# Scores of a sparse-attention mixer over 128 rows instead of 64, scalings moved from GpSimd to VectorE, and a shorter skip at the end

## The chip, the cores and the metric

The kernel runs on one core of one Trainium2 chip. Its time is the device time of one launch in microseconds; shown are the median and the spread of several runs. The engines are TensorE (PE; its weight loads are PEld), VectorE (DVE), ScalarE (ACT), GpSimd (POOL) and SyncE (SP), which issues the DMAs.

## The reference

Two layers work on 256 tokens of width 1024, each a mixer and a mixture of 16 experts, with a layer norm behind each. The first mixer (stick-breaking attention beside a state-space model) is not touched. The second is a sparse attention of 16 heads of 64 with 4 groups of keys. It has three branches: compressed blocks, selected blocks, and a window. With 256 tokens all blocks are selected and the window covers everything, so the last two are plain causal attention over their own keys (ks, kw) and values (vs, vw).

```python
scale = d ** -0.5                                  # d = 64
s = jnp.einsum('bqgrd,bkgd->bqgrk', qb, kb).astype(jnp.float32) * scale
s = jnp.where(mask[None, :, None, None, :], s, NEG)
p = jax.nn.softmax(s, axis=-1)
o_w = jnp.einsum('bqgrk,bkgd->bqgrd', p.astype(vb.dtype), vb)
...
g = jax.nn.sigmoid(gate.astype(jnp.float32)).reshape(B, L, G, R, 3).astype(x.dtype)
o = g[..., 0:1] * o_c + g[..., 1:2] * o_s + g[..., 2:3] * o_w
return o.reshape(B, L, H * d) @ w_out
```

The expert layers multiply all 256 tokens with the three matrices of each of the 16 experts (6 MB an expert), gated by the router.

## The kernel before

The large products of the mixers are of 32-bit floats in the type fp32r, with each operand split into a high part, which that type holds, and the low rest; they are the sums of high times high, high times low and low times high. Weights come in tiles of 1 MB (128 x 2048) that SP's queue loads into the buffers of the class `u` (20 of them) as these come free (`issue`, L131 to L148). Other classes are `s` (3), `b2` (15 small ones) and eight banks of PSUM, of which `mm` and `acc` have four each. Temporary tiles take their buffers from the same classes as weights, so that a longer-lived temporary is one weight tile less.

The mixer's attention is the generator `attend` (L1558). Step n computes the scores of head n (`head`, L1490), transposes the probabilities of head n - 2 (`turn_p`, L1525), and on every other step the values of a pair of heads (`values`, L1538). A head has two blocks of queries, t = 0 (128 keys) and t = 1 (256 keys), each for the two branches b at once. The queries are turned (`q_turn`, L1391) for eight heads at a time, into the tiles `qq[0]` and `qq[1]`: rows of 64 with the high part, the other 64 with the low part. So L1504, over 128 rows, gives q_high times k_high plus q_low times k_high in one matmul, since the keys' high part `kk` stands in both halves; L1505 adds q_high times k_low with 64 rows of q and the tiles `kl`; L1506 adds the causal mask through a matmul with the identity in bf16. VectorE then takes the maxima (L1507), ScalarE the exponentials and their sums (L1510), VectorE the reciprocals (L1513) and their product with the gates (L1515). The probabilities are scaled by these: for t = 0 on VectorE (L1522, one instruction a branch, 128x128), for t = 1 on GpSimd (L1519, one for both branches, 128x512). `PSC` holds that choice. `turn_p` transposes both, the first with L1529 and the second with L1535.

The first few steps of the attention lie between other jobs: the projections of the mixer (`mm3`, L203 to L205) and the compressed branch (L1455 to L1482). `q_turn(1)` and `cmp(1)` are called between the steps for heads 7 and 8. Each engine executes its own instructions in order. The calls don't set that order alone: the framework's scheduler lays them out by what they wait for. Buffers are given out in the order of calls.

`body` (L1722) runs the whole network once with a limit of 64 tokens per expert. Then every engine loads the largest count of tokens (L1726) and compares (L1728). If it is over the limit, the body of the `If` computes everything anew without the limit. In the runs here that body is skipped. The end block behind it (L1741) waits for all transfers and lets the engines meet.

Of the kernel before, what the change touches and what calls it, by code (L numbers as in the profile page):

```python
# [19 lines left out]
P = 128  # L20
# [18 lines left out]
WARM0 = 5  # L39
WARM2 = 2  # L40
LAG = 2
PSC = (lambda h: False, lambda h: True)
OV = 3
LATE = (8, 10)
LATE_S = 11
# [6 lines left out]
class K:  # L52
# [17 lines left out]
    def restart(self, full):  # L70

        self.full = full
        self.plan, self.tiles, self.late, self.late_s, self.in_s, self.last = [], [], [], [], [], []
        self.left = []
        self.issued = self.used = 0
        self.cap = 0
        self.rest = self.n0 = None
        self.mark = None
        self.loads = None
        self.behind = self.cut = self.tail = None  # L80
        self.staged, self.to_split, self.ahead = [], 0, 2
# [49 lines left out]
    def issue(self, cap=None):  # L131

        self.cap = self.cap if cap is None else cap
        while self.issued < len(self.plan):
            if self.issued - self.used - sum(self.used <= i < self.issued for i in self.left) >= self.cap:
                break
            if self.issued in self.left:
                self.tiles.append(None)
                self.issued += 1
                continue  # L140
            t = (self.s if self.issued in self.in_s else self.u)()
            n = 1024 if self.issued in self.last else 2048
            for c in range(0, 2048, n):
                d = self.loads = self.nc.sync.dma_start(t[:, c:c + n], self.plan[self.issued][:, c:c + n])
                if self.mark is not None:
                    self.follow(d, self.mark)
            self.tiles.append(t)
            self.issued += 1  # L148

    def issue_late(self):  # L150

        i = self.late.pop(0)
        self.tiles[i] = [self.b2() for _ in range(4)]
        for j, t in enumerate(self.tiles[i]):
            self.nc.sync.dma_start(t, self.plan[i][:, j * 512:j * 512 + 512])

    def issue_s(self):

        i = self.late_s.pop(0)
        self.tiles[i] = t = self.s()  # L160
        self.nc.sync.dma_start(t, self.plan[i])

    def unit(self):
        t = self.tiles[self.used]
# [60 lines left out]
    def pack(self, name, dt, parts, t=None):  # L225

        if t is None:
            t = self.const.tile([P, sum(math.prod(sh) for sh in parts)], dt, name="c_" + name)
            setattr(self, name, t)
        d = self.nc.sync.dma_start(t, self.a[name])  # L230
        if self.loads is not None:
            self.follow(d, self.loads)
        o, r = 0, []
        for sh in parts:
            m = math.prod(sh)
            v = t[:, o:o + m]
            if len(sh) > 1:
                ax = "abcd"[:len(sh)]
                v = v.rearrange(f"p ({' '.join(ax)}) -> p {' '.join(ax)}", **dict(zip(ax, sh)))
            r.append(v)  # L240
            o += m
        return r
# [95 lines left out]
    def ln_transpose(self, li, n, store=None):  # L338

        nc = self.nc  # L340
        hT = self.u([P, KC, T])
        for k in range(KC):
            pt = self.acc() if k in (4, 5) else self.mm()
            for t in range(2):
                nc.tensor.transpose(pt[:, t * P:(t + 1) * P], n[:, t, k * P:(k + 1) * P], self.ident)
            self.scaled(hT[:, k], pt[:, 0:T], li, k, k % 2)
            if store is not None and k % 2:
                nc.sync.dma_start(store[:, k - 1:k + 1], hT[:, k - 1:k + 1])
        return hT

    def scaled(self, o, x, li, k, on_act):
# [305 lines left out]
    def s5_tables(self, load_x, room):  # L657
# [4 lines left out]
        small = lambda t, j: t[:, j * 512:j * 512 + 512].rearrange("p (a r h) -> p a r h", a=NP, r=2)  # L662
        par = us[:, 1344:1392].rearrange("p (x a) -> p x a", x=3)
        c8 = us[:, 1392:1424]
        nc.sync.dma_start(us[:, 1344:1424], self.a["s5_par"])
        load_x()
        bc = ua[:, 0:1024].rearrange("p (x a r h) -> p x a r h", x=2, a=NP, r=2)
        nc.sync.dma_start(bc, self.a["s5_bc"])
        lr, li, ldt = par[:, 0], par[:, 1], par[:, 2]
        cols = us[:, 0:960].rearrange("p (n a) -> p n a", a=NP)  # L670
        ints = us.bitcast(I32)[:, 1424:1456].rearrange("p (n a) -> p n a", a=NP)
# [185 lines left out]
    def s5_kernel(self, ca, bd):  # L857

        nc, s5 = self.nc, self.s5
        nc.gpsimd.memset(bd, 0.0)  # L860
        for g in range(2):
            s = slice(g * 64, g * 64 + 64)
            nc.scalar.activation(bd[s, :, :, g * 16:g * 16 + 16], s5["bb"][s], AF.Copy)
        pk = self.mm()
        for k4 in range(4):
            for ri in range(2):
                for q in range(4):
                    pr = k4 * 4 + q
                    nc.tensor.matmul(pk[q * 32:q * 32 + 32, k4 * P:k4 * P + P], bd[:, pr, ri],
                                     ca[ri][:, pr].rearrange("p d h -> p (d h)"), start=(ri == 0), stop=(ri == 1),  # L870
                                     skip_group_check=True, tile_position=(0, q * 32))
        ks = self.b2([P, 4, P])
        nc.scalar.activation(ks.rearrange("p k n -> p (k n)"), pk, AF.Copy)
        nc.gpsimd.tensor_tensor(ks[:, :, 0:16], ks[:, :, 0:16], self.s5dd, ALU.add)
        kds = []
        for kh in range(2):
            kd = self.drp.tile([16, 16, P], F32, name=f"kd{kh}")
            nc.sync.dma_start(kd.rearrange("h (g k) n -> g h (k n)", g=8),
                                ks[:, kh * 2:kh * 2 + 2].rearrange("p k n -> p (k n)"))
            kds.append(kd)  # L880
        return kds

    def s5_toeplitz(self, kds, kts):

        for kt, kd in zip(kts, kds):
            for j in range(8):
                n = 16 * (8 - j)
                self.nc.sync.dma_start(kt[j * 16:j * 16 + 16, :, P - n:P], kd[:, :, 0:n])

    def s5_transpose(self, x, o):  # L890

# [176 lines left out]
    def mixer0(self):  # L1068
# [5 lines left out]

        def load_x():
            t = self.u()
            half = lambda c: nc.sync.dma_start(t[:, c * 1024:c * 1024 + 1024], self.plan[0][:, c * 1024:c * 1024 + 1024])
            for k in range(0, KC, 2):
                nc.sync.dma_start(xT[:, k:k + 2], self.a["xT"][:, k:k + 2])
                if k == 0:  # L1080
                    half(0)
            half(1)
            self.tiles.append(t)
            self.issued += 1
# [16 lines left out]
        def u_out(j):  # L1101
            def f(ps):
                nc.scalar.activation(uS[:, :, j], ps[:, 0:T].rearrange("p (c i) -> p i c", i=8), AF.Copy)
                if j == 3:
                    ud = self.drp.tile([8, P, P], F32, name="ud")
                    nc.sync.dma_start(ud.rearrange("j a n -> a j n"), uS.rearrange("p j k c -> p j (k c)"))
                    nc.sync.dma_start(U.rearrange("p g k c -> p (g k c)"), ud.rearrange("j (h g) n -> (j h) (g n)", h=16))
            return f

        bbp = [self.u([P, 16, 8, 16]) for _ in range(2)]  # L1110
# [190 lines left out]
    def mixer1(self, hT):  # L1301
# [43 lines left out]
        kk = self.u([P, 2, 2, 2, T], F32R)  # L1345
        vh = self.u([P, 2, 1024])
        V = vh[:, 0].rearrange("p (t n) -> p t n", t=2)
        kl = [self.b2((P, 2, T), F32R) for _ in range(2)]
        rows = (slice(0, 64), slice(64, P))

        turned = {}
# [4 lines left out]
        def k_turn(t):  # L1356
            pt = self.turn(turned["k", t]).rearrange("p (b j) n -> p j b n", b=2)
            n = slice(t * P, t * P + P)
            for c, s in enumerate(rows):
                nc.scalar.activation(kk[s, c, :, :, n], pt[s], AF.Copy)  # L1360
                for j in range(2):
                    v.tensor_tensor(kl[j][s, :, n], pt[s, j], kk[s, c, j, :, n].bitcast(F32), ALU.subtract)
                nc.scalar.activation(kk[rows[1 - c], c, :, :, n], pt[s], AF.Copy)

        js = [self.job_T(xs, window(i)) for i in (1, 2, 3)] + self.jobs_tok(xs, k_out, self.acc)
# [121 lines left out]
        hd = {}  # L1487

        def head(i, c):
            j, s = i // 4, slice(c * 64, c * 64 + 64)  # L1490
            h = i * 2 + c
            if c == 0:
                hd["PT"] = self.u()
            PT = hd["PT"][:, 0:1536].rearrange("p (c b n) -> p c b n", c=2, b=2)[:, c]
# [4 lines left out]
            for t in range(2):  # L1499
# [2 lines left out]
                z3 = z[:, 0:2 * n].rearrange("p (b n) -> p b n", b=2)  # L1502
                q = qq[j][:, c, i % 4, t * P:t * P + P]
                nc.tensor.matmul(z3, q, kk[:, c, j, :, 0:n], start=True, stop=False, skip_group_check=True)  # L1504
                nc.tensor.matmul(z3, q[s], kl[j][s, :, 0:n], start=False, stop=False, skip_group_check=True)  # L1505
                nc.tensor.matmul(z3[:, :, t * P:t * P + P], self.identb, self.caus, start=False, stop=True, skip_group_check=True)  # L1506
                v.tensor_reduce(mx[:, 2 * t:2 * t + 2], z3, AX.X, ALU.max, negate=True)  # L1507
                p_ = self.b2((P, 2, T)) if t else p0
# [5 lines left out]
            s2 = sm.rearrange("p (t b) -> p t b", t=2)  # L1514
            v.tensor_tensor(s2, s2, gt[:, :, h, 1:3], ALU.mult)  # L1515
            for t in range(2):
                x, n, pool = pr[t], P * (t + 1), PSC[t](h)
                if pool:
                    nc.gpsimd.tensor_tensor(x, x, sm[:, 2 * t:2 * t + 2, None].broadcast_to([P, 2, n]), ALU.mult)  # L1519
                    continue  # L1520
                for b in range(2):
                    v.tensor_scalar(x[:, b], x[:, b], sm[:, 2 * t + b:2 * t + b + 1], None, ALU.mult)  # L1522
            hd[h] = (pr, PT)

        def turn_p(h):  # L1525
# [196 lines left out]
def body(ctx, tc, a, out):  # L1722
# [2 lines left out]
    network(k, a, out)  # L1725
    v = nc.values_load(k.mxi[0:1, 0:1], min_val=0, max_val=T,  # L1726
                       skip_runtime_bounds_check_because="a count of tokens, only compared")
    with tc.If(v > LIMIT):  # L1728

        k.restart(True)  # L1730
        network(k, a, out)
# [20 lines left out]
```

## Time and profile before

| | us |
|---|---|
| median of 3 runs | 756.65 |
| the three runs | 756.65, 756.63, 759.73 |
| the profiled execution | 759.68 |
| its span, from first to last instruction | 757.8 |
| TensorE busy | 733.8 (97%) |
| VectorE busy | 333.1 (44%) |
| ScalarE busy | 207.5 (27%) |
| GpSimd busy | 46.8 (6%) |
| DMA | 241 MB, mean 318 GB/s |

The profile is of one execution, and busy times are modelled for TensorE: a new matmul starts before the one ahead of it has ended, so the distance of two starts is what one costs in a stream. The lengths of VectorE's and ScalarE's instructions overlap a little in the same way. "Idle before, releaser" names what an engine waited for. A shared line of weights (L144, L203) collects all uses of a helper, so that stretches of time are a better cut than lines. The granted clock is 1.00 at 2.4 GHz and 0.50 at 1.2 GHz.

### The profile page before, as it was taken

To read this page: it belongs to the slowest core of one execution; us is meant where nothing else is said; L and a number is where in the kernel's file an instruction comes from. 1 tells how busy PE (TensorE), PEld (TensorE's weight loads), DVE (VectorE), ACT (ScalarE), POOL (GpSimd) and SP (SyncE) were. 2 spreads that over 40 slices of the span, in tenths; PEclk is the share of its full clock that TensorE was granted. 3 is DMA by queue.
4 is the path that set the end of the run, shared out by engine and by line. 5 is a ranking of instruction groups with operands and counts; after the bars stand their busy time and mean duration, and the time that the engine had idled before them with its cause. 6 is when DMAs were issued, how large, how long until landed. Compare 5 with 4: busy or idle time off the path is not lost. (4 is left out here: it accounts for less than half of the span.)

```text
span 757.8 us, 10531 instructions
## 1 busy us (share of the span) xinstructions
PE 733.8 (97%) x4115; PEld 413.9 (55%) x4115; DVE 333.1 (44%) x849; ACT 207.5 (27%) x422; POOL 46.8 (6%) x45
## 2 busy tenths in 40 slices
PE   7999999999999999999999999999999999999993
PEld 6588777634334335334878665687535335343332
DVE  9995667512112112115855897835212112221123
ACT  1345443212101001003534675732211001011002
POOL 2010000002000000000020241300002000000000
PEclk9999999999999999999999998999999999999998
DMA  8838999799999999999982100398799999999941
GB/s 321 299 119 147 398 372 402 256 347 387 381 425 421 421 422 421 420 416 422 420 338 106 57 1 1 135 387 308 233 376 395 393 421 421 422 420 421 421 185 60
DMA packets 42539, 241.00 MB, mean 318 GB/s; under 512 B 8144, under 2 KB 9680, under 8 KB 15568
## 3 DMA queue, kind: packets, MB, share of 16 engines
q1 hardware_dynamic: 42480, 240.23, 80.7%
q8 instruction: 34, 0.56, 0.3%
q14 instruction: 25, 0.20, 0.1%
HBM read 238.38 MB, written 1.84 MB: 317 GB/s over the span
## 5 line engine op out<-in xcount | busy, mean ns | idle before, releaser
L493 PE MATMUL mm<-u,s 128*64 128x512 f32 x960 | 214.3, 595 | 0.0
L493 PEld LDWEIGHTS mm<-u,s 128*64 128x64 f32 x960 | 66.7, 137 | 129.6 <-issue 122.3
L523 PE MATMUL mm<-u,b 128*64 128x512 f32 x512 | 113.1, 593 | 0.0
L528 ACT ACTIVATE b<-mm,gslot 128x512 fp32r<-128x512 f32 x32 | 22.0, 687 | 259.0 <-PE mm L523 259.0
L529 DVE SCALAR_TENSOR_TENSOR b<-mm,gslot,b 128x512 fp32r<-128x512 f32 x32 | 24.0, 751 | 146.2 <-ACT b L528 146.2
L523 PEld LDWEIGHTS mm<-u,b 128*64 128x64 f32 x512 | 36.3, 137 | 72.0 <-issue 70.8
L195 DVE TENSOR_TENSOR s<-u,s 128x1024 fp32r<-128x1024 f32 x37 | 45.8, 1248 | 27.9 <-ACT s L192 26.3
L572 DVE TENSOR_TENSOR b<-b,mm 128x256 f32<-128x256 f32 x32 | 12.0, 417 | 92.0 <-PE mm L493 92.0
L192 ACT ACTIVATE s<-u 128x1024 fp32r<-128x1024 f32 x37 | 38.7, 1056 | 42.0 <-PE acc L205 28.9
L986 PE MATMUL mm<-u,u 128*128 128x256 f32 x208 | 46.7, 382 | 2.5 <-DMA u<-w_in 2.4
L986 PEld LDWEIGHTS mm<-u,u 128*128 128x128 f32 x208 | 38.9, 190 | 9.6 <-issue 2.4
L354 ACT ACTIVATE s<-mm,c_k_all 128x256 f32<-128x256 f32 x32 | 18.1, 564 | 81.8 <-PE mm L469 81.8
L469 PE MATMUL mm<-b,u 128*128 128x256 f32 x160 | 39.0, 325 | 0.0
L203 PE MATMUL acc<-s,u 128*128 128x512 f32 x96 | 38.0, 396 | 0.5 <-ACT u L1206 0.5
L205 PE MATMUL acc<-s,u 128*128 128x512 f32 x96 | 37.8, 394 | 0.0
L204 PE MATMUL acc<-s,u 128*128 128x512 f32 x96 | 37.5, 391 | 0.0
L534 PE MATMUL acc<-b,b 128*128 128x512 f32 x128 | 33.6, 399 | 0.1
L469 PEld LDWEIGHTS mm<-b,u 128*128 128x128 f32 x160 | 29.9, 190 | 6.4 <-issue 4.9
L592 DVE COPY b<-mm 128x512 f32<-128x512 f32 x16 | 11.1, 692 | 46.4 <-PE mm L591 46.2
L356 DVE TENSOR_SCALAR s<-mm,c_k_all 128x256 f32<-128x256 f32 x32 | 16.8, 542 | 22.9 <-PE mm L469 22.7
L534 PEld LDWEIGHTS acc<-b,b 128*128 128x128 f32 x128 | 22.5, 189 | 8.0 <-issue 3.2
L469 PE MATMUL mm<-b,s 128*128 128x256 f32 x96 | 23.5, 286 | 0.0
(312 smaller groups left out, 998.8 us busy)
## 6 DMA issues: line engine op xcount, KB each, us to landing
u<-moe SPq DMA_DIRECT2D x180, 1024.0 KB, 12.5
u<-w_in SPq DMA_DIRECT2D x26, 1024.0 KB, 16.2
u<-w_in SPq DMA_DIRECT2D x10, 512.0 KB, 6.9
s<-moe SPq DMA_DIRECT2D x4, 1024.0 KB, 5.7
b<-moe SPq DMA_DIRECT2D x16, 256.0 KB, 8.1
u<-moe SPq DMA_DIRECT2D x8, 512.0 KB, 16.9
u<-xT SPq DMA_DIRECT2D x4, 256.0 KB, 5.6
out<-u SPq DMA_DIRECT2D x4, 256.0 KB, 4.4
```

Source lines behind the costliest of these rows:

```text
L192: a = self.nc.scalar.activation(s[:, 0], x, AF.Copy)
L195: self.mark = self.nc.vector.tensor_tensor(s[:, 1], x, s[:, 0].bitcast(F32), ALU.subtract)
L203: mm(o, l[0], r[0], start=first, stop=False, skip_group_check=True)
L204: mm(o, l[0], r[1], start=False, stop=False, skip_group_check=True)
L205: self.tail = mm(o, l[1], r[0], start=False, stop=last, skip_group_check=True)
L469: nc.tensor.matmul(pg[:, 0:T], x[:, t, k * P:(k + 1) * P], g.bitcast(F32) if m == 1 else g, start=(i == 0), stop=(i == 2 * m - 1))
L493: self.mark = nc.tensor.matmul(h[c * 64:(c + 1) * 64], xe[:, k, e + c], w[c], start=(k == 0), stop=(k == KC - 1))
L523: self.mark = nc.tensor.matmul(y[c * 64:(c + 1) * 64], hx[:, f, c * 64:(c + 1) * 64], w[:, c * 512:c * 512 + 512], start=(f == 0), stop=(f ...
L528: nc.scalar.activation(yh, y, AF.Copy, scale=gs)
L529: nc.vector.scalar_tensor_tensor(yl, y, gs, yh.bitcast(F32), ALU.mult, ALU.subtract)
L534: self.tail = nc.tensor.matmul(out[half][t], sT[:, t * P:(t + 1) * P], yy, start=False, stop=(p == 7 and j == 1), skip_group_check=True)
L986: self.mark = self.nc.tensor.matmul(ps, w[:, k * P:k * P + P], xT[:, k], start=(k == 0), stop=(k == KC - 1))
```

## The change

Four things change; the lines of the new kernel are up to 4 smaller behind L1363 (L1522 becomes L1518, L1529 L1525, L1535 L1531, L1741 L1737) or one larger around L1397 and L1456.

1. `kl` becomes one `u` tile of the same shape as `kk`, and its other halves are set to zero by two memsets on GpSimd. L1505 uses all 128 rows of q, the low part of q meeting zeros. The subtraction in `k_turn` is one for both groups of keys.
2. `PSC` is gone: VectorE scales both blocks of queries.
3. In the body of the `If`, the DMAs are issued by GpSimd's queue (`self.q`).
4. The `If` gets `preferred_fallthrough_block=False`, which puts the block that skips the body right behind the compare.

```diff
+        self.q = self.nc.gpsimd if full else self.nc.sync
...
-                d = self.loads = self.nc.sync.dma_start(t[:, c:c + n], self.plan[self.issued][:, c:c + n])
+                d = self.loads = self.q.dma_start(t[:, c:c + n], self.plan[self.issued][:, c:c + n])
...
-        kl = [self.b2((P, 2, T), F32R) for _ in range(2)]
+        kl = self.u([P, 2, 2, 2, T], F32R)
+        for c in range(2):
+            nc.gpsimd.memset(kl[(1 - c) * 64:(1 - c) * 64 + 64, c].bitcast(F32), 0.0)
...
-                for j in range(2):
-                    v.tensor_tensor(kl[j][s, :, n], pt[s, j], kk[s, c, j, :, n].bitcast(F32), ALU.subtract)
+                v.tensor_tensor(kl[s, c, :, :, n], pt[s], kk[s, c, :, :, n].bitcast(F32), ALU.subtract)
...
-                nc.tensor.matmul(z3, q[s], kl[j][s, :, 0:n], start=False, stop=False, skip_group_check=True)
+                nc.tensor.matmul(z3, q, kl[:, c, j, :, 0:n], start=False, stop=False, skip_group_check=True)
...
-                x, n, pool = pr[t], P * (t + 1), PSC[t](h)
-                if pool:
-                    nc.gpsimd.tensor_tensor(x, x, sm[:, 2 * t:2 * t + 2, None].broadcast_to([P, 2, n]), ALU.mult)
-                    continue
                 for b in range(2):
-                    v.tensor_scalar(x[:, b], x[:, b], sm[:, 2 * t + b:2 * t + b + 1], None, ALU.mult)
+                    v.tensor_scalar(pr[t][:, b], pr[t][:, b], sm[:, 2 * t + b:2 * t + b + 1], None, ALU.mult)
...
-    with tc.If(v > LIMIT):
+    with tc.If(v > LIMIT, preferred_fallthrough_block=False):
```

The first place is TensorE around the turn of the second eight heads' queries, where L1298 transposes the turned queries' source, and the long scores of head 7 (`acc_3445`) follow. Before:

```order
L1298 MATMUL mm_3418<-c_k_all,b_554_3282 128x128 [waits PE_49]
L1298 MATMUL mm_3418<-c_k_all,b_554_3282 128x128 x3
L1298 MATMUL mm_3427<-c_k_all,b_556_3289 128x128 [waits DVE_49]
L1298 MATMUL mm_3427<-c_k_all,b_556_3289 128x128 x3
L1504 MATMUL acc_3445<-u_2582,u_2875 128x512
L1505 MATMUL acc_3445<-b_454_2584,u_2875 128x512
L1506 LDWEIGHTS c_k_bits
L1506 MATMUL acc_3445<-c_k_bits 128x2x128
L1529 MATMUL mm_3458<-c_k_all,u_3296 128x128 [waits DVE_49,Activation_49]
L1529 MATMUL mm_3458<-c_k_all,u_3296 128x128 [waits DVE_49]
L1535 MATMUL mm_3462<-c_k_all,b_571_3355 128x128 [waits DVE_49,Pool_49]
```

After (`acc_3449` are head 7's long scores, `acc_3500` the first of head 8):

```order
L1298 MATMUL mm_3422<-c_k_all,b_553_3283 128x128 [waits PE_49,Pool_49]
L1298 MATMUL mm_3422<-c_k_all,b_553_3283 128x128 x3
L1298 MATMUL mm_3431<-c_k_all,b_555_3290 128x128 [waits Activation_49,Pool_49]
L1298 MATMUL mm_3431<-c_k_all,b_555_3290 128x128 x3
L1505 MATMUL acc_3449<-u_2584,u_2872 128x512
L1506 LDWEIGHTS c_k_bits
L1506 MATMUL acc_3449<-c_k_bits 128x2x128
L1525 MATMUL mm_3463<-c_k_all,u_3297 128x128 [waits DVE_49]
L1525 MATMUL mm_3463<-c_k_all,u_3297 128x128
L1531 MATMUL mm_3467<-c_k_all,b_570_3357 128x128 [waits DVE_49]
L1531 MATMUL mm_3467<-c_k_all,b_570_3357 128x128 x3
L1504 MATMUL acc_3500<-u_2582,u_2873 128x256 [waits DVE_49]
```

The second score matmul of head 7, of 128 rows now, stands behind L1298 and without its L1504, which has moved further ahead; the first scores of head 8 still wait for VectorE.

On ScalarE at the same place, before (L1396 copies the high part of the second queries, L1510 are the exponentials, L1536 copies the transposed probabilities):

```order
L1510 ACTIVATE u_3373,sm_586_3437<-acc_3438,mx_585_3436 128x128 [waits DVE_49,Pool_49]
L1396 ACTIVATE u_2876<-mm_3418 64x4x128 [waits PE_49,Activation_49]
L1396 ACTIVATE u_2876<-mm_3427 64x4x128 [waits PE_49]
L1510 ACTIVATE u_3373,sm_586_3437<-acc_3438,mx_585_3436 128x128
L1536 ACTIVATE u_3296<-mm_3462 128x2x256 [waits PE_49]
L1396 ACTIVATE u_2876<-mm_3418 64x4x128 [waits DVE_49]
L1396 ACTIVATE u_2876<-mm_3427 64x4x128 [waits DVE_49]
```

After, where the copy is L1397:

```order
L1510 ACTIVATE u_3376,sm_585_3441<-acc_3442,mx_584_3440 128x128 [waits DVE_49]
L1510 ACTIVATE u_3376,sm_585_3441<-acc_3442,mx_584_3440 128x128
L1397 ACTIVATE u_2873<-mm_3422 64x4x128 [waits PE_49]
L1397 ACTIVATE u_2873<-mm_3431 64x4x128
L1532 ACTIVATE u_3297<-mm_3467 128x2x256 [waits PE_49]
L1397 ACTIVATE u_2873<-mm_3422 64x4x128 [waits DVE_49]
L1397 ACTIVATE u_2873<-mm_3431 64x4x128 [waits DVE_49]
```

The first copy now has both exponentials of head 7's short block ahead of it and waits for TensorE alone. The tile that it writes has another buffer than before: the new `kl` has the one that `qq[1]` had, and `qq[1]` has that of `qq[0]`, whose last reader is L1505 of head 7, and so the copy waits for that.

The third place is SP at the end. Before, the body of the `If` stands behind the compare, and the block that skips it behind the body:

```order
L348 DMA out<-u_13172 128x512 [waits DMAHW6_49,DVE_49,Activation_49]
L348 DMA out<-u_13172 128x512 [waits DMAHW7_49,DVE_49,Activation_49]
L348 DMA out<-u_13172 128x512 [waits DMAHW0_49,DVE_49,Activation_49]
L348 DMA out<-u_13172 128x512 [waits DMAHW1_49,DVE_49,Activation_49]
L1728 UNCONDITIONAL_BRANCH
L1728 UNCONDITIONAL_BRANCH [waits DMAHW0_49,DMAHW1_49,DMAHW2_49,DMAHW3_49,DMAHW4_49,DMAHW5_49,DMAHW6_49,DMAHW7_49]
```

After, from the stores of the result on, the whole skip (SP has 571 instructions in the program before and 295 after):

```order
L348 DMA out<-u_5266 128x512 [waits DMAHW2_49,DVE_49,Activation_49]
L348 DMA out<-u_5266 128x512 [waits DMAHW3_49,DVE_49,Activation_49]
L348 DMA out<-u_5266 128x512 [waits DMAHW4_49,DVE_49,Activation_49]
L348 DMA out<-u_5266 128x512 [waits DMAHW5_49,DVE_49,Activation_49]
L1722 TENSOR_LOAD mxi [waits DVE_49]
L1724 COMPARE_AND_BRANCH
L1724 UNCONDITIONAL_BRANCH
```

The skip has come forward to stand right behind the compare and has no waits; the body on SP has shrunk from 290 rows of this kind to 15, as its DMAs went to GpSimd's queue. TensorE, ScalarE and VectorE keep their long bodies and still jump over them.

## Rows read from the trace of the kernel before

**Rows 1.** The windows by stretch: start:end, length, busy us of each engine, clock, DMA share.
```profile
426.00:454.50 28.50, 28.50 (x171) 18.42 (x170) 26.25 (x69) 20.80 (x75) 9.59 (x11) 1.00 0.08 34
458.18:465.00 6.82, 6.82 (x28) 3.63 (x29) 5.08 (x14) 2.76 (x13) 1.04 (x1) 0.50 0.00 0
467.40:498.00 30.60, 30.37 (x210) 20.52 (x209) 21.34 (x58) 18.97 (x69) 7.30 (x7) 1.00 0.40 158
600.00:727.00 127.00, 127.00 (x623) 52.96 (x620) 22.99 (x53) 13.13 (x22) 0.00 (x0) 1.00 1.01 421
```

**Rows 2.** The timeline of TensorE, one head's scores: start, length, engine, line, operation.
```profile
435.81 0.36 PE L1504 MATMUL acc<-u,u 128*128 128x256 f32 x1
...
436.86 0.50 PE L1505 MATMUL acc<-b,u 64*128 64x512 f32 x1
...
437.33 0.48 PE L203 MATMUL mm<-s,u 128*128 128x512 f32 x1
```

**Rows 3.** The same view, matmuls of 128 rows.
```profile
410.28 0.39 PE L203 MATMUL acc<-s,u 128*128 128x512 f32 x1
410.51 0.40 PE L204 MATMUL acc<-s,u 128*128 128x512 f32 x1
```

**Rows 4.** The same view, where the second queries are turned.
```profile
454.50 0.60 PE L1535 MATMUL mm<-c_k_all,b 128*128 128x128 f32 x4
456.10 0.38 PE L1504 MATMUL acc<-u,u 128*128 128x256 f32 x1 [1.00 <-DVE u L1397]
...
456.94 0.64 PE L1455 MATMUL mm<-u,b 128*32 128x256 f32 x8
```

**Rows 5.** Groups by line and shape, VectorE, 426 to 498 us: busy, mean ns.
```profile
L1522 DVE TENSOR_SCALAR u<-u,sm 128x128 f32<-128x128 f32 x32 | 17.9, 593 | 0.1
```

**Rows 6.** The timeline of VectorE: a pair of scalings, and one alone.
```profile
438.75 0.96 DVE L1522 TENSOR_SCALAR u<-u,sm 128x128 f32<-128x128 f32 x2
...
466.54 0.19 DVE L1522 TENSOR_SCALAR u<-u,sm 128x128 f32<-128x128 f32 x1
466.65 0.18 DVE L1474 TENSOR_TENSOR cmx<-cmx,b 128x16 f32<-128x16 f32 x1
```

**Rows 7.** The timeline of GpSimd beside that pair.
```profile
438.40 1.04 POOL L1519 TENSOR_TENSOR b<-b,sm 128x512 f32<-128x512 f32 x1 [1.75 <-DVE sm L1515]
```

**Rows 8.** Single lines: count, duration in ns min/median/max, first and last start.
```profile
L1062 DVE TENSOR_SCALAR b<-b x3: 295/426/428, 97.2 to 396.8; 128x512 f32<-128x512 f32 x2, 128x256 f32<-128x256 f32 x1
...
L1362 DVE TENSOR_TENSOR b<-mm,u x8: 404/418/429, 394.0 to 397.5; 64x256 fp32r<-64x256 f32 x8
...
L1396 ACT ACTIVATE u<-mm x8: 574/592/592, 422.4 to 456.7; 64x512 fp32r<-64x512 f32 x8
...
L1397 DVE TENSOR_TENSOR u<-mm,u x8: 675/684/693, 424.2 to 458.0; 64x512 fp32r<-64x512 f32 x8
```

**Rows 9.** Waits of SP: for what, us in total, times, longest.
```profile
SPq L144 <- DVE u L1530: 58.8, 2, 57.8
...
SPq L1728 <- SPq L1728: 3.2, 1, 3.2
```

**Rows 10.** The program's end by line: SP, TensorE, VectorE, and the stores.
```profile
L1728 SPq EVENT_SEMAPHORE  x8: 17/17/17, 753.3 to 753.8; - x8
...
L1728 PEldq COMPARE_BRANCH  x1: 4542/4542/4542, 747.9 to 747.9; - x1
...
L1728 SPq COMPARE_BRANCH  x1: 50/50/50, 750.0 to 750.0; - x1
...
L1728 DVEq EVENT_SEMAPHORE  x1: 21/21/21, 753.1 to 753.1; - x1
...
L1741 SPq EVENT_SEMAPHORE  x14: 17/28/28, 753.9 to 757.7; - x14
...
L348 SPq DMA_DIRECT2D out<-u x4: 343/376/396, 747.2 to 748.6; - x4
...
DMA to landing us min/median/max: 2.2/4.4/4.5
```

More of the change, by code (lines that the diff above doesn't have):

```diff
@@ L41 @@
 LAG = 2
-PSC = (lambda h: False, lambda h: True)
 OV = 3
@@ L154, in issue_late @@
         for j, t in enumerate(self.tiles[i]):
-            self.nc.sync.dma_start(t, self.plan[i][:, j * 512:j * 512 + 512])
+            self.q.dma_start(t, self.plan[i][:, j * 512:j * 512 + 512])
     def issue_s(self):
@@ L160, in issue_s @@
         self.tiles[i] = t = self.s()
-        self.nc.sync.dma_start(t, self.plan[i])
+        self.q.dma_start(t, self.plan[i])
     def unit(self):
@@ L229, in pack @@
             setattr(self, name, t)
-        d = self.nc.sync.dma_start(t, self.a[name])
+        d = self.q.dma_start(t, self.a[name])
         if self.loads is not None:
@@ L347, in ln_transpose @@
             if store is not None and k % 2:
-                nc.sync.dma_start(store[:, k - 1:k + 1], hT[:, k - 1:k + 1])
+                self.q.dma_start(store[:, k - 1:k + 1], hT[:, k - 1:k + 1])
         return hT
@@ L664, in s5_tables @@
         c8 = us[:, 1392:1424]
-        nc.sync.dma_start(us[:, 1344:1424], self.a["s5_par"])
+        self.q.dma_start(us[:, 1344:1424], self.a["s5_par"])
         load_x()
         bc = ua[:, 0:1024].rearrange("p (x a r h) -> p x a r h", x=2, a=NP, r=2)
-        nc.sync.dma_start(bc, self.a["s5_bc"])
+        self.q.dma_start(bc, self.a["s5_bc"])
         lr, li, ldt = par[:, 0], par[:, 1], par[:, 2]
@@ L877, in s5_kernel @@
             kd = self.drp.tile([16, 16, P], F32, name=f"kd{kh}")
-            nc.sync.dma_start(kd.rearrange("h (g k) n -> g h (k n)", g=8),
+            self.q.dma_start(kd.rearrange("h (g k) n -> g h (k n)", g=8),
                                 ks[:, kh * 2:kh * 2 + 2].rearrange("p k n -> p (k n)"))
@@ L887, in s5_toeplitz @@
                 n = 16 * (8 - j)
-                self.nc.sync.dma_start(kt[j * 16:j * 16 + 16, :, P - n:P], kd[:, :, 0:n])
+                self.q.dma_start(kt[j * 16:j * 16 + 16, :, P - n:P], kd[:, :, 0:n])
     def s5_transpose(self, x, o):
@@ L1076, in load_x @@
             t = self.u()
-            half = lambda c: nc.sync.dma_start(t[:, c * 1024:c * 1024 + 1024], self.plan[0][:, c * 1024:c * 1024 + 1024])
+            half = lambda c: self.q.dma_start(t[:, c * 1024:c * 1024 + 1024], self.plan[0][:, c * 1024:c * 1024 + 1024])
             for k in range(0, KC, 2):
-                nc.sync.dma_start(xT[:, k:k + 2], self.a["xT"][:, k:k + 2])
+                self.q.dma_start(xT[:, k:k + 2], self.a["xT"][:, k:k + 2])
                 if k == 0:
@@ L1105, in f @@
                     ud = self.drp.tile([8, P, P], F32, name="ud")
-                    nc.sync.dma_start(ud.rearrange("j a n -> a j n"), uS.rearrange("p j k c -> p j (k c)"))
-                    nc.sync.dma_start(U.rearrange("p g k c -> p (g k c)"), ud.rearrange("j (h g) n -> (j h) (g n)", h=16))
+                    self.q.dma_start(ud.rearrange("j a n -> a j n"), uS.rearrange("p j k c -> p j (k c)"))
+                    self.q.dma_start(U.rearrange("p g k c -> p (g k c)"), ud.rearrange("j (h g) n -> (j h) (g n)", h=16))
             return f
@@ L1489, in head @@
         def head(i, c):
-            j, s = i // 4, slice(c * 64, c * 64 + 64)
-            h = i * 2 + c
+            j, h = i // 4, i * 2 + c
             if c == 0:
```

## The prediction, made before the changed kernel was run

> **What bounds the kernel now.** I read the windows by stretch first. In the second mixer's attention (426 to 498 us) TensorE is busy 28.50 of 28.50 us in the first half and 30.37 of 30.60 in the last; the reader is to see that no other engine or queue is as full, and that only 454.5 to 467.4 us has an idle us [rows 1]. VectorE comes close in the first half, 26.25 of 28.50, and stays at 21.34 of 30.60 later. The DMA share is small here. So a shorter TensorE stream shortens the attention, as long as VectorE follows. The timeline of TensorE then prices one head's scores [rows 2, 3], those of VectorE and GpSimd the scalings [rows 5 to 7], and the instructions of the program's last lines the end [rows 10]. The profiled execution took 759.68 us (span 757.8, 1.9 around it); the three timed runs 756.65, 756.63 and 759.73. The profile has one stretch at half clock, 6.82 us at 0.50 (1.2 of 2.4 GHz), right after TensorE sat idle 1.00 us at 456.10 [rows 1, 4]. At half clock 6.82 us do the work of 3.41, so it cost 3.4 us, which is about what parts the third timed run and the profile from the other two. I read the median as an execution without it.
>
> **Scores over 128 rows.** A head's six score matmuls (256, 256, 256, then 512, 512, 256 columns) take from 435.81 to 437.33: 1.52 us; from the L1505 of 64 rows and 512 columns to what follows its mask, 0.47 us [rows 2]. 128-row matmuls of 512 columns, each with its own weights, start 0.23 us apart [rows 3]. The six have 2048 columns, four times 512: 0.92 us at that pace. Saved per head: 0.60 us, for 16 heads 9.6. The other end is nothing saved, should the 1.52 come from the short mask matmul and not from the 64 rows; I take 0.60, being nearest to the row of equal width and columns [rows 3]. Two rules of the Trainium skill part here: "TensorE: Matmul & The Clock Gate", "Why this matters for your kernels", has a matmul of few rows take as long as one of 128, by which alone the edit would be worth 0; "TensorEngine Tiling (Array Packing)", "Key Properties", has every change between tilings of the array drain TensorE, by which the switch costs and goes. The trace, 1.52 us where equal columns take 0.92, goes with the second.
>
> **Scalings on VectorE.** GpSimd loses 16 of 1.04 us [rows 7]. VectorE gets 32 of 128x256, 0.295 us each by the one 128x256 TENSOR_SCALAR of L1062 [rows 8]. It also gets something back: its own two scalings of 128x128 a head cost 17.9 us in all, 1.12 a head, and 0.96 a pair beside GpSimd's product at 438.40, but 0.19 for one at 466.54, where GpSimd does nothing and the next instruction starts 0.11 later [rows 5 to 7]. Alone, the four of a head should start in 2 x 0.11 + 2 x 0.21 = 0.64 us (0.295 less the same overlap of 0.08). VectorE thus gains about 0.4 a head (1.12 - 0.64, less some joints). Ends: 0.5 gained, or 0.5 lost when sharing with GpSimd is not what made 1.12.
>
> **The attention summed.** First half, 8 heads: TensorE 28.5 - 8 x 0.6 = 23.7, VectorE 26.25 - 8 x 0.4 = 23.0. Two engines equally full that hand work to each other don't reach the larger sum; I take 25.0, so -3.5 (ends -4.8 and +1.8). Last 6 heads: TensorE bounds alone, -3.6. Between them lies the turn of the second half of the queries. The new zero-padded key tile takes a u buffer, so that both qq tiles share one, and ScalarE's first L1397 for the second waits for the last score matmul of head 7. Behind that wait stand ScalarE's other copies and VectorE's four subtractions, on which the scores of heads 8 and 9 wait. From there: ScalarE 0.59 and hand-overs of some 0.2, then on VectorE four L1398 (4 x 0.69 [rows 8]), four scalings (0.64) and a reduction (0.69, taken like L1397 of as many columns), 4.9 us. TensorE has meanwhile six transposes and a mask (some 0.75, by the 0.60 of four [rows 4]), the short and the long score group (0.35 and 0.58 by the pace above) and L1456 (0.64 by [rows 4]), 2.3 us. Idle 2.6 instead of 1.00: +1.6; two heads save 1.2; net +0.4 (ends -1.2 and +2.5). Attention: -3.5 + 0.4 - 3.6 = -6.7 us.
>
> **What lies beside.** The keys' subtractions, 8 of 0.42 us, become 4 of 512 columns and some 0.69 [rows 8], like L1397 of the same shape: less in sum, and 30 us ahead of the attention; two memsets stand early on GpSimd, behind nothing that anyone waits for: 0, and by the nearest row, a GpSimd pass over as many elements, 1 us each if the buffer came free late. The loads on SP keep their order. They hang on buffers that the attention frees (58.8 us of SP's waiting is for L1530 [rows 9]) and so move ahead with it, and what the attention gains passes through to the second MoE.
>
> **The end.** SP's compare is at 750.0, its next instructions are the eight waits at 753.3 to 753.8, with only itself to blame for 3.2 us [rows 9, 10]. The last store is issued at 748.6 and lands about 4.4 later, 753.1; TensorE's compare takes 4.5 us, and VectorE is through at 753.1 [rows 10]. The end block starts on SP at 753.9 and its last instruction is at 757.7: 3.8 us, though its instructions take 17 or 28 ns. The change leaves SP neither the eight waits nor the long jump. Yet the store's landing is still waited for in the end block, and the others still jump far, so nothing ends before 753.1. Sure is 753.9 - 753.1 = 0.8, less 0.2 for a hand-over: 0.6. At the other end the whole stall of SP goes, and the 3.8 us shrink by as much as the 3.2 that SP lost at its branch: 3.5 in sum, at most. Nearest to the row of 3.2 us is that SP's stall in the end block is of the same kind and mostly goes: I take 2.8. The Trainium skill, "Runtime: NRT & Kernel Launch", "Instruction fetch mechanics", says that a jump out of the fetched pages has to wait for a fetch, and that SP's new short jump would not: by that alone 3.5. TensorE's 4.5 us at its compare agree.
>
> **Sum.** -6.7 - 2.8 = -9.5: from the profiled 759.68 to 750.2 with the half-clock stretch in it, from the median of 756.65 to 747.2. I forecast 747.2; its own range is 744.5 to 749.
>
> **Rivals.**
> The half clock stays or comes back: 750.2 (749 to 752). For it: the idle at the turn grows from 1.0 to 2.6 us. Against: two of three timed runs seem free of it.
> SP's stall comes back elsewhere in the end block: 0.6 instead of 2.8, 749.4. For it: 753.9 to 757.7 of short instructions is unexplained by any row.
> VectorE becomes the bound: if its scalings don't get quicker without GpSimd's, it has 26.25 + 8 x 0.5 = 30.3 us in the first half where 28.5 were, +1.8; attention +1.8 + 0.4 - 3.6 = -1.4, with the end 752.4. Against it stands the 0.19 at 466.54.
> DMA bounds the second MoE: share 1.01 from 600 to 727 [rows 1]. If the loads did not move ahead, the attention's gain would be waited away: 756.65 - 2.8 = 753.9. Against it: SP's 58.8 us behind L1530.
> Slower: TensorE, thinner and stopped more often, runs the attention at half clock. Each us at 0.50 costs half a us; 9.5 is used up by 19 us, three stretches like the one, and 27 us make it slower beyond doubt: with four, 747.2 + 4 x 3.4 = 760.8. For it: the one drop followed an idle us. Against: TensorE stays over 90% busy, and its 0.23 idle us from 467.4 to 498 left the clock at 1.00 [rows 1]. The Trainium skill, "TensorE: Matmul & The Clock Gate", "A second HAM failure mode", tells of a kernel whose short stops between groups of matmuls made the clock go back and forth; in the 72 us of attention here it changed once and came back.
>
> **Numbers.** A measurement of this kernel tells 0.5%, 3.8 us, from no change; same is 752.9 to 760.4. Forecast 0.43, half clock 0.22, SP's stall 0.13, VectorE 0.10 (half of it under 752.9), DMA 0.07, slower 0.05. Faster: 0.43 + 0.22 + 0.13 + 0.05, and 0.02 of the DMA case, 0.85; same 0.10; slower 0.05. Range 743.5 to 753.0: the low end has 9.6 for the attention and 3.5 at the end, the high end takes in VectorE as the bound and leaves out the DMA and the slower case and the tails of the others.
>
> **What would show it.** Right: L1504 to the next group at about 0.92 us a head; L1518 at 0.19 and 0.30 us each and no pairs of 1 us; a wait of TensorE for L1398 above 1 us; SP's end block right behind its compare, and about 2 us from the last store's landing to the last instruction. Wrong: score matmuls still 0.3 and 0.45 apart; waits of TensorE for L1518 at every head; waits for DMA in the second MoE; more than one stretch of 0.50; a gap on SP behind its branch as long as before.

## The result, and the profile after

The changed kernel takes 751.78 us in the median of five runs (750.41 to 752.16), beside 756.74 for the kernel before in the same session (756.63 to 761.17). The ratio is 0.9917, with a 95% interval of 0.9888 to 0.9945. The medians differ by 5.0 us. Forecast were 747.2, 9.5 us less than before, and a range of 743.5 to 753.0. So the time lies within the range, but outside the forecast's own part of it (744.5 to 749). The profiled execution took 751.73 us, with a span of 750.0.

An execution loses more or less time to stretches at half clock: of 35 runs of the kernel before in the session of the first experiments, 21 took 756.1 to 756.9 us at a mean clock of 0.995 to 0.997, and 14 took 759.1 to 761.2 at 0.989 to 0.992.

The windows by stretch of the profile after, cut at the first scores of head 0, of head 8, of head 10, and at the output projection; the second row is the stretch of half clock. Columns as in [rows 1]:

```profile
427.37:455.87 28.50, 26.54 (x174) 18.67 (x172) 26.04 (x81) 21.10 (x75) 2.77 (x4) 0.94 0.12 38
447.18:450.60 3.42, 3.24 (x12) 2.16 (x12) 3.29 (x13) 2.83 (x13) 0.00 (x0) 0.50 0.00 0
455.87:464.73 8.86, 7.35 (x60) 4.58 (x61) 8.58 (x23) 5.37 (x19) 0.00 (x0) 1.00 0.00 0
464.73:493.68 28.95, 28.23 (x212) 20.34 (x210) 21.28 (x82) 19.86 (x73) 0.00 (x0) 1.00 0.37 146
```

Before, the same four marks were at 426.37, 456.10, 467.36 and 498.02 us. To see those stretches without the half clock, here is e3_skip, an experiment told below, which has the old attention and had no half clock there (the whole attention, heads 8 and 9, the rest):

```profile
426.78:495.52 68.74, 67.52 (x441) 43.90 (x440) 57.82 (x152) 46.49 (x164) 19.53 (x20) 1.00 0.21 83
456.51:464.87 8.36, 8.36 (x60) 4.83 (x61) 8.07 (x21) 5.98 (x21) 1.78 (x2) 1.00 0.00 0
464.87:495.52 30.65, 30.42 (x211) 20.57 (x210) 22.14 (x63) 19.03 (x69) 7.61 (x8) 1.00 0.40 158
```

The last column of the table takes off what the half clock can have cost at most, half of its 3.41 us.

| stretch | before | before, no half clock (e3) | after | after, less at most half of 3.41 |
|---|---|---|---|---|
| start to first score | 426.37 | 426.78 | 427.37 | |
| heads 0 to 7 | 29.73 | 29.73 | 28.50 | 26.8 |
| heads 8, 9 | 11.26 | 8.36 | 8.86 | 8.9 |
| rest to the projection | 30.66 | 30.65 | 28.95 | 29.0 |
| projection to TensorE's load at the end | 249.24 | 249.25 | 249.21 | |
| from there to the end of the span | 10.53 | 7.55 | 7.10 | |

The old half-clock stretch cost 11.26 - 8.36 = 2.9 us (the prediction priced it at 3.4). The attention has lost 2.4 us against an old one without it (68.74 to 66.31), up to 4.1 at equal clock. The rest of the program, the second MoE in it, has not taken anything back: its 249.2 us are the same.

The scores, on the timeline of TensorE (answers to [rows 2]):

```profile
435.18 0.36 PE L1504 MATMUL acc<-u,u 128*128 128x256 f32 x1
...
435.86 0.40 PE L1505 MATMUL acc<-u,u 128*128 128x512 f32 x1
...
436.14 0.47 PE L203 MATMUL mm<-s,u 128*128 128x512 f32 x1
```

Head to next work is 0.96 us instead of 1.52. That step came out as forecast (0.92).

The scalings, in the groups of VectorE (answer to [rows 5]) and on its timeline (answer to [rows 6]):

```profile
L1518 DVE TENSOR_SCALAR b<-b,sm 128x256 f32<-128x256 f32 x32 | 9.7, 346 | 0.0
L1518 DVE TENSOR_SCALAR u<-u,sm 128x128 f32<-128x128 f32 x32 | 7.8, 279 | 0.1
```

```profile
472.10 0.47 DVE L1518 TENSOR_SCALAR u<-u,sm 128x128 f32<-128x128 f32 x2
472.49 0.61 DVE L1518 TENSOR_SCALAR b<-b,sm 128x256 f32<-128x256 f32 x2
473.02 0.42 DVE L1526 COPY u<-mm 128x256 f32<-128x256 f32 x1
```

The two kinds overlap a little, so that they can't be added. The window of L1518 alone counts each moment once:

```profile
427.37:493.68 66.31, 16.32 (x64) 0.97 0.21 80
```

So both kinds together are busy 16.3 us, where the one kind of before was busy 17.9. The four of a head start over 473.02 - 472.10 = 0.92 us. The forecast had 0.64: the narrow ones last 279 ns on average and not 188, the wide ones 346 and not 295. VectorE got 1.5 us lighter in 16 heads, 0.1 a head, where 0.4 were forecast.

The turn of the second queries (answers to [rows 4]) has three waits, 2.1 us, where one of 2.6 was forecast:

```profile
455.87 0.38 PE L1504 MATMUL acc<-u,u 128*128 128x256 f32 x1 [0.62 <-DVE u L1398]
...
457.71 0.64 PE L1456 MATMUL mm<-u,b 128*32 128x256 f32 x8 [1.22 <-DVE u L1398]
...
459.79 0.64 PE L1456 MATMUL mm<-u,b 128*32 128x256 f32 x8 [0.29 <-DVE u L1398]
```

A wait that was not forecast stands ahead of the attention:

```profile
406.36 0.44 PE L1404 MATMUL mm<-c_k_all,b 128*128 128x128 f32 x2 [0.65 <-ACT u L1446]
...
427.37 0.28 PE L1504 MATMUL acc<-u,u 128*128 128x256 f32 x1
```

The scheduler has put the keys' turn on ScalarE behind two weight splits (L1362 at 400 us, L1360 of before at 393), and TensorE waits 0.65 us for the compressed branch behind it. The first score starts at 427.37, 1.0 us later than before; the part of it that is not this wait was not traced.

The end, by line (answers to [rows 10]), and SP's wait in it:

```profile
L1724 PEldq COMPARE_BRANCH  x2: 95/2302/4510, 743.5 to 743.8; - x2
...
L1724 SPq COMPARE_BRANCH  x2: 38/46/53, 745.6 to 745.7; - x2
...
L1737 SPq EVENT_SEMAPHORE  x14: 17/28/28, 745.9 to 749.9; - x14
...
L1737 SPq DRAIN  x3: 7/7/7, 749.1 to 749.4; - x3
```

```profile
SPq L1737 <- DMA out<-u: 2.5, 2, 1.9
```

SP's end block starts at 745.9, right behind its two branches at 745.6 and 745.7, and waits 2.5 us for the last stores (issued up to 744.4, landing up to 4.6 later). TensorE's jump still takes 4.5 us, but beside that wait. The tail is 3.4 us shorter.

### The profile page after: what moved, and what is told of

It reads as the page before. It is cut to its first block, busy times and chain, and to the rows that moved or that the text cites. A ratio compares the mean times of both kernels' runs of the same rounds, so it can differ in the third digit from the quotient of the medians.

```text
span 750.0 us, 10494 instructions
## 1 busy us (share of the span) xinstructions
PE 726.7 (97%) x4115; PEld 412.8 (55%) x4115; DVE 330.8 (44%) x877; ACT 208.0 (28%) x422; POOL 31.9 (4%) x31
```

## The experiments

**One part of the change at a time.** e1 to e4 are the kernel before with one edit each, in one session, where that kernel took 756.72.

e1_scores has the `kl` tile, the memsets, the subtraction and the 128-row matmul (the last is shown):

```diff
...
-                nc.tensor.matmul(z3, q[s], kl[j][s, :, 0:n], start=False, stop=False, skip_group_check=True)
+                nc.tensor.matmul(z3, q, kl[:, c, j, :, 0:n], start=False, stop=False, skip_group_check=True)
```

> The kernel before with the scores over 128 rows alone; GpSimd still scales half of the probabilities and the end is the old one. My theory (TensorE bounds the attention, VectorE is close behind it): a head's scores start about 0.96 us apart, the attention gains 2 to 4 us at equal clock, 753.5 us (752.5 to 755). Rival (VectorE beside GpSimd is the bound as soon as TensorE gets shorter, so that the scores are worth nothing without the scalings): 755.7 to 757, with TensorE's waits for L1522 or for GpSimd's L1519 at most heads.

Measured 755.28 us, ratio 0.9964 (0.9948 to 0.998). Its attention, and the first eight heads of it:

```profile
427.41:492.67 65.26, 60.72 (x441) 42.12 (x440) 57.34 (x152) 46.41 (x164) 19.52 (x20) 1.00 0.21 81
427.41:456.42 29.01, 25.81 (x174) 17.61 (x172) 28.12 (x72) 22.23 (x80) 10.16 (x11) 1.00 0.10 38
```

68.74 has become 65.26, 3.5 us, with VectorE busy 28.12 of 29.01 us in the first part. So TensorE's shorter scores count, though the first part, where VectorE is nearly full, gained least (29.73 to 29.01). My range holds the attention; the time came out just above its range. The late keys took 1.0 us back, and ten of the twelve runs had a mean clock of 0.993 or 0.994, where the profiled one (753.91 us) had 0.996.

e2_scale has the scalings alone:

```diff
-PSC = (lambda h: False, lambda h: True)
+PSC = (lambda h: False, lambda h: False)
```

> The kernel before with all scalings on VectorE alone; scores over 64 rows and the old end. My theory (TensorE is the bound of before, so that a lighter VectorE gives nothing): 756.2 us (755.6 to 757), VectorE's four scalings 0.28 and 0.35 us each. Rival (the scalings' chain over GpSimd held the attention back): 753.5 to 755.

757.70 us, ratio 1.0006 (0.9985 to 1.0026). The profile, without half clock, has an attention that is 2.6 us longer than 68.74 (the second row is the part behind head 10):

```profile
426.45:497.77 71.32, 69.42 (x441) 44.53 (x440) 55.88 (x184) 46.27 (x164) 2.78 (x4) 1.00 0.19 73
466.10:497.77 31.67, 31.37 (x211) 20.97 (x210) 20.97 (x80) 19.29 (x71) 0.00 (x0) 1.00 0.37 139
```

So alone the move is a loss there, and neither theory had that. Why is open. It shows how little a full TensorE says: behind head 10 the same 211 matmuls are busy 31.37 of 31.67 us here and 30.42 of 30.65 in e3. TensorE's busy time grows with the stretch, so that a busy share near one doesn't show that TensorE sets the pace. Its end was 2.3 us shorter than that of before (8.2 us), with the same skip; SP's last block ran through in 1.6 us, where it took 3.8 before [rows 10], with a gap of over 2 us:

```profile
L1741 SPq EVENT_SEMAPHORE  x14: 17/28/28, 753.7 to 755.3; - x14
```

That end makes up for most of the longer attention. What makes the gap come and go is open.

e3_skip has both edits of the skip; e4_fall only the order of the blocks:

```diff
-    with tc.If(v > LIMIT):
+    with tc.If(v > LIMIT, preferred_fallthrough_block=False):
```

> The kernel before with the changed skip alone (both the order of the blocks and the DMAs of the skipped body on GpSimd's queue). My theory (the end lost 3.4 us in the profile after): 753.3 us (752.8 to 753.9), with SP's end block right behind its compare. Rival (the end's gain in the profile after came from stores that landed earlier there, and the store's landing is all that counts): 755.5 to 756.3.

> The kernel before with the order of the blocks alone: the skip stands right behind the compare, with its eight waits, but the body on SP keeps its 290 rows, so that the end block is far away. My theory (SP's long jump costs, not the waits): 756.0 us (755.5 to 756.6). Rival (the waits, or their place behind the jump, cost): about the same as with both, 753.3.

e3_skip: 754.03 us, ratio 0.9962 (0.9942 to 0.9983), the tail 3.0 us shorter than before. e4_fall: 758.76 us, ratio 1.002 (0.9998 to 1.0042). Both theories of e4 were wrong; its profile has a tail of 12.4 us:

```profile
L1728 SPq EVENT_SEMAPHORE  x8: 17/17/17, 750.3 to 753.6; - x8
...
L1728 SPq COMPARE_BRANCH  x2: 38/46/53, 750.2 to 753.7; - x2
...
L1741 SPq EVENT_SEMAPHORE  x14: 17/28/28, 756.7 to 759.8; - x14
```

The eight waits now come first (750.3 to 753.6, until the stores have landed), then a second branch at 753.7, and the end block at 756.7. The jump still costs 3.0 us. Before, it lay beside the landing of the stores; here it comes after it. The order of the blocks alone is worth nothing, or less; with it, the short body on SP, by the DMAs on GpSimd's queue, takes the jump away (the short body without the order was not run). How much of the 3.0 us of e3 that explains is open: e2 lost 2.3 us of its end with the old skip, as its gap went, and e3's end is only 0.6 us shorter than e2's.

**What is the move of the scalings worth in the whole?** e5_scores_skip is e1 with e3, so the change without that part.

> The changed kernel with GpSimd scaling the long halves again, so scores over 128 rows and the new skip, without the move of the scalings. My theory (the scalings on VectorE are worth next to nothing, since its four now start 0.92 us apart a head where the two of before took about 1.1, and the segments of the profiles differ by 0.65 us at equal clock): 751.0 to 752.6, most likely 752.2, no more than 0.7 from the changed kernel. Rival (the move of the scalings is what lets VectorE follow the shorter scores, and made the three edits worth more together than apart): 753.4 or more.

752.31 us (751.04 to 753.99), against 751.78 (750.41 to 752.16). That is 4.4 less than the kernel before in its session (756.75), where e1 and e3 alone had given 1.4 and 2.7. In its profile:

```profile
428.43:493.84 65.41, 60.85 (x442) 42.11 (x440) 57.36 (x152) 46.41 (x164) 19.53 (x20) 1.00 0.21 80
```

```profile
L1524 DVE TENSOR_SCALAR u<-u,sm 128x128 f32<-128x128 f32 x32 | 18.0, 597 | 0.0
```

The narrow scalings cost 18.0 us again beside GpSimd. Moving the wide ones is worth half a us in the medians, which the runs don't tell from nothing; the gain is that of the scores and the end.

**The turn.** e6_b2 puts the low keys into four small buffers, so that the query tiles don't share one; e7_turn gives GpSimd the wide scalings of heads 6 and 7; e8_both does both.

```diff
-        kl = self.u([P, 2, 2, 2, T], F32R)
+        kl = [[self.b2((P, 2, T), F32R) for _ in range(2)] for _ in range(2)]
...
```

```diff
             for t in range(2):
+                if t and h in (6, 7):
+                    nc.gpsimd.tensor_tensor(pr[t], pr[t], sm[:, 2:4, None].broadcast_to([P, 2, T]), ALU.mult)
+                    continue
```

> The changed kernel with the zero-padded low keys in four small buffers instead of one of the weights' buffers, so that the two query tiles don't share one. My theory (the shared buffer makes TensorE wait at the turn to the second eight heads): the waits for L1398 there go from 0.6 + 1.2 + 0.3 to about 1.0 in all, time 750.8. Rival (VectorE's queue of subtractions and scalings sets that wait): 751.8, waits as in the changed kernel.

> The changed kernel with the long halves of heads 6 and 7 alone scaled by GpSimd, those whose scalings stand among the subtractions of the second queries. My theory of the turn by its rival (VectorE's queue sets the wait): the waits for L1398 lose 0.5 to 1.0 us, time 751.1. If the shared buffer sets it: no change, 751.8. If GpSimd's product slows VectorE's narrow scalings beside it again to 0.5 us each, the gain is eaten: 751.8 with such scalings in the trace.

> Both edits at the turn: the low keys in four small buffers, and the long halves of heads 6 and 7 scaled by GpSimd. If the shared buffer and VectorE's queue each make a part of the turn's waits: 750.9 (750.4 to 751.5), the waits for L1398 about 0.6 in all. If they are one wait counted twice: 751.4 to 751.9.

Times: 751.90 (750.37 to 752.71), 751.45 (750.74 to 753.44) and 752.10 us (751.02 to 752.86): none differs from the changed kernel. TensorE's waits at the turn and the attention, of e6 and then of e7:

```profile
PE acc L1506 <- DVE u L1400: 1.0, 1, 1.0
```

```profile
427.01:493.15 66.14, 62.80 (x441) 43.68 (x440) 55.44 (x184) 46.01 (x164) 2.77 (x4) 0.97 0.21 80
```

```profile
PE mm L1456 <- DVE u L1398: 1.0, 2, 0.7
...
PE acc L1504 <- DVE u L1398: 0.6, 1, 0.6
```

```profile
426.95:492.25 65.30, 61.52 (x441) 42.74 (x440) 55.25 (x180) 46.32 (x164) 4.86 (x6) 1.00 0.22 81
```

In e6 the wait for the second queries (L1400 there) is 1.0 us instead of 2.1, in e7 1.6. Each edit shortens it, so both causes are real. But the time doesn't follow: e6's attention had the 3.41 us of half clock, e7's none, and e8 had two such stretches (66.98 us at a mean clock of 0.95). What a shorter wait gave was less than what the clock moved, or came back as a wait elsewhere. Nor do the two add up: e8's wait is 1.2 us, where 0.6 were expected of both together.

```profile
PE acc L1506 <- DVE u L1400: 1.2, 1, 1.2
```

```profile
427.42:494.40 66.98, 63.22 (x442) 44.06 (x440) 55.89 (x180) 46.03 (x164) 4.85 (x6) 0.95 0.20 77
```

**What bounds the attention now?** e9_light leaves out the wide scalings, e10_short leaves out L1505.

```diff
             for t in range(2):
+                if t:
+                    continue
```

> The changed kernel without the scaling of the long halves (left out; those probabilities stay unscaled), so that VectorE has 32 instructions of 0.35 us less and GpSimd gets none. From the first scores to the output projection the changed kernel took 66.3 us, 64.6 without its stretch of half clock. If VectorE bounds the attention now: 62.5 us or less at full clock. If TensorE does: 64 to 64.6.

> The changed kernel without L1505 (the product of the queries' high part with the keys' low part is left out), 0.35 us of TensorE a head, 5.6 in all. From the first scores to the output projection: if TensorE bounds the attention now, 59 to 60 us at full clock; if VectorE does, 63.5 or more, with TensorE's waits for VectorE and ScalarE grown by the rest.

The attention of e9, and the part of it behind head 10; then the same of e10, with the first eight heads between:

```profile
428.66:489.16 60.50, 59.10 (x441) 42.41 (x440) 47.58 (x152) 46.28 (x164) 2.78 (x4) 1.00 0.22 84
462.23:489.16 26.93, 26.93 (x211) 19.82 (x210) 17.12 (x65) 20.08 (x73) 0.00 (x0) 1.00 0.37 148
```

```profile
427.45:494.41 66.96, 61.40 (x410) 40.88 (x408) 55.64 (x184) 45.52 (x164) 2.78 (x4) 0.95 0.20 77
427.45:456.84 29.39, 25.67 (x157) 16.87 (x155) 26.81 (x85) 21.05 (x76) 2.78 (x4) 0.94 0.07 29
465.57:494.41 28.84, 27.34 (x200) 18.97 (x198) 21.75 (x81) 19.17 (x72) 0.00 (x0) 1.00 0.38 149
```

With 32 instructions less on VectorE, 60.5 us; with 5.6 us less on TensorE, 66.96, or 63.5 if its two half-clock stretches of 3.41 us cost half of their length. By parts it is plainer: e10's first eight heads take 29.39 us (28.50 in the changed kernel, with the same 3.41 us of half clock), and its part behind head 10 takes 28.84 (28.95). So TensorE's work no longer bounds the attention. The wide scalings on VectorE do, behind head 10 most clearly: without them that part takes 26.93 us, all of it with TensorE busy. That is not the same as a full VectorE: there it is busy only 21.28 of 28.95 us in the changed kernel. What seems to count is that the scalings stand in the way from a head's scores to its transposes; this is argued, and e11 below bears it out. e10 took 752.34 us in its one run.

e9's changed numbers sent more tokens to an expert than the limit, so the body of the `If` ran, and the kernel took 11855 us. e12_taken is the kernel before with the same part left out:

> The kernel before without the scaling of the long halves (left out, as in e9_light), whose numbers send more tokens to an expert than the limit, so that the body of the If runs; here its DMAs are on SP's queue. In e9_light, with GpSimd's queue, that took 11855 us and the DMAs ran at 40 GB/s. If GpSimd's queue makes it slow: 3000 to 5000 us, with over 100 GB/s in the body. If the body is slow by its own work: 11000 or more.

11832 us. The queues of e9, then of e12 (packets, MB, share of the DMA engines' time):

```profile
q0 software_dynamic: 232784, 642.74, 16.5%
q1 hardware_dynamic: 42480, 240.23, 5.1%
```

```profile
q0 software_dynamic: 196608, 403.05, 11.4%
q1 hardware_dynamic: 84672, 479.93, 10.3%
```

So my theory fell: the body used GpSimd's queue for most of its data already (403 MB), and 240 MB more there go with 23 us of 11.8 ms, in one run of each. The changed skip costs next to nothing when it isn't skipped.

**A version from this.** e11_pool gives GpSimd all scalings:

```diff
-                for b in range(2):
-                    v.tensor_scalar(pr[t][:, b], pr[t][:, b], sm[:, 2 * t + b:2 * t + b + 1], None, ALU.mult)
+                n = P * (t + 1)
+                nc.gpsimd.tensor_tensor(pr[t], pr[t], sm[:, 2 * t:2 * t + 2, None].broadcast_to([P, 2, n]), ALU.mult)
```

> The changed kernel with all scalings on GpSimd, one instruction a half (128x256 and 128x512), and none on VectorE. My theory (VectorE bounds the attention now; without its wide scalings it took 60.5 us instead of 64.6): VectorE loses both kinds, 17.5 us in all, and nothing of its kind shares with GpSimd's; GpSimd has some 1.6 us a head, 26 of 62. From the first scores to the output projection 61 to 63 us at full clock, time 749.0 (748.0 to 750.5). Rival (the longer way over GpSimd, from the gates' product to the transposes, makes TensorE wait instead): 751.5 to 753, with TensorE's waits for the products on GpSimd at most heads.

750.65 us (750.21 to 752.51), ratio 0.9898 (0.9868 to 0.9927). It is the fastest in the medians, by 1.1 us over the changed kernel, within the spread of the two, and lies between the two ranges that were expected. Its attention, the part behind head 10, and TensorE's wait for GpSimd in all of the attention:

```profile
426.87:492.12 65.25, 61.00 (x441) 41.81 (x440) 43.42 (x120) 46.75 (x164) 30.43 (x36) 1.00 0.22 84
461.18:492.12 30.94, 28.35 (x211) 19.66 (x209) 14.87 (x49) 20.10 (x73) 12.88 (x16) 1.00 0.36 141
```

```profile
PE mm L1531 <- POOL b L1518: 2.5, 5, 0.6
```

VectorE is down to 43.4 us. The first ten heads take 34.3 us (37.4 in the changed kernel, with half clock), the rest 30.9 (29.0). GpSimd isn't full there either (12.88 of 30.94 us), and VectorE has half of the stretch free: where heads follow without other work between them, GpSimd's 1.77 us a head (1.10 and 0.67) make the way to the transposes too long. GpSimd for the first ten heads and VectorE for the rest was not tried.

## Why the prediction was right, and where its size was off

It was right in direction and within its range, for 5.0 us where 9.5 were forecast. The range held the time because it takes in the rivals: 751.78 lies in that of the rival with half clock (749 to 752), whose mechanism made at most 1.7 of the 4.5 us that were missing. The end gave 0.6 more than its term and so hid a part of the miss, which was luck.

- Scores over 128 rows: right. 0.96 us a head for a forecast 0.92. The rule of the Trainium skill ("TensorEngine Tiling (Array Packing)", "Key Properties") that a change of tiling drains TensorE fits; by the other ("TensorE: Matmul & The Clock Gate", "Why this matters for your kernels"), nothing would have been gained.
- "VectorE thus gains about 0.4 a head": this step failed. It gained 0.1, 16.3 us for 17.9. I priced the wide scaling by one L1062 and the narrow one by the one that stood between smaller instructions. The measured gain lies between the ends of that term, 0.5 gained and 0.5 lost.
- "Last 6 heads: TensorE bounds alone, -3.6": failed. Measured -1.7, and e10 shows that TensorE's work is not the bound there (28.84 us for 28.95 with less of it), e9 that the wide scalings on VectorE are (26.93). I read a busy TensorE as the bound; e2 shows that it can be busy 31.37 of 31.67 us without being it. The rival with VectorE as the bound had the right engine, but not the place, as I put its price into the first eight heads, and not the reason, a load of 30.3 us: VectorE had 26.04 of 28.50 us there and 21.28 of 28.95 in the last heads.
- The first eight heads: at most -2.9 for a forecast -3.5.
- The turn: right in the sum. +0.5 for +0.4, with 2.1 us of waits for 2.6, both from the shared buffer (e6) and VectorE's queue (e7). The split from the first eight heads is loose, as a wait at the turn can fall ahead of the first score of head 8 or behind it (e1: 1.9 us ahead of it, and 7.4 us for heads 8 and 9).
- "What lies beside: 0": failed by 1.0 us, the late turn of the keys. Why the scheduler puts it later is open. TensorE's wait of 0.6 us there is in every profile with the scores over 128 rows, also with small buffers for the low keys (e6), and in none of e2, e3 and e4.
- The end: -3.4 for -2.8, with its cause only in part shown. e4 shows what I had not weighed: a jump beside a transfer's landing costs next to nothing. Up to 2.3 of the 3.4 us are the gap in the old end block, which was gone in e2 with the old skip too; whether the new skip took it away is not shown. The upper end of that term is also added up wrong, as 0.6 and 3.2 make 3.8, not 3.5.
- The clock: I took none of the half-clock stretches into the forecast. Four of the five runs have a mean clock of 0.996, as the profile with one stretch of 3.41 us, which at most costs 1.7. The run at 0.998 took 750.41.

In sum: -9.5 + 1.9 (last heads) + 0.6 (first heads) + 0.1 (turn) + 1.0 (keys) - 0.6 (end) + 1.7 (clock) = -4.8, for -5.0 measured. The first heads and the clock are known only together, as 2.3.

## What to carry to other kernels

Where the second engine is 92% busy beside a bound one, ask what an instruction costs there in a stream of its own kind before counting on its relief; a faster first engine only hands the bound over. A wait that goes is worth what it stuck out beyond the other waits: order decides, and the same jump costs next to nothing beside a landing and 3 us behind it. Busy shares (TensorE 62 of 66 us, VectorE 56) don't name the bound: leaving out work on each suspect in turn showed in two runs that TensorE's work no longer was it and the scalings were. A third run, with the scalings on an engine that had room, showed that the length of the way counts beside the load.

## What the runs showed of the hardware

- A VectorE scaling of 128x128 took 279 ns on average in a stream of scalings, 188 between other instructions (one case), and 597 on average in e5, where GpSimd scales the long halves.
- The stretches of half clock in the attention lasted 3.41 us (the changed kernel, e6, e8, e10) or 6.83 us (before, e4). One of 6.83 us cost 2.9 us. The same waits of TensorE stood ahead of such a stretch in one profile and not in another: 1.0 us at the turn with one behind it in before and e4 and none in e2 and e3; 0.5 and 0.6 us some 10 us earlier with one in the changed kernel and none in e7. In e1 a wait of 1.9 us left the clock at 1.00.
- A far jump cost SP 2.9 to 3.2 us (e2, e4, before) and TensorE 4.3 to 4.5 us.
- With two 64-row matmuls among six, a head's scores took 1.52 us; the same columns, all over 128 rows with zeros, took 0.96.
